# A decoder trunk's FFNs: beginning each down pass with the up pass's last pair, straight from SBUF

## Chip, cores, metric

One core of a Trainium2 chip runs the whole program as one launch. The metric is the device time of that core in microseconds (us), the median of several executions.

## What is computed

One decoder layer for 1024 prompt tokens and 64 sample tokens of width 1024, all in float32: a SwiGLU feed-forward network (FFN) with 2816 hidden columns, a mixer of four gated-MLP groups and four mLSTM heads, and a second FFN, each followed by a layer norm over a scaled residual.

```python
def swiglu(x, wg, wu, wd):
    return (jax.nn.silu(x @ wg) * (x @ wu)) @ wd

def decoder_layer(x, conv_buf, C0, n0, m0, prm):
    x = layer_norm(ALPHA * x + 0.5 * swiglu(x, f1_wg, f1_wu, f1_wd), ln1_g, ln1_b)
    z = x @ w_in + b_in
    u, v, q, k, vm, o, ig, fg = jnp.split(z, SPLIT_POINTS, axis=-1)
    gm, vn = chunk_gmlp(gelu(u), gelu(v), gm_ln_g, gm_ln_b, gm_ws, gm_bs)
    qk = jax.nn.silu(causal_dwconv(concat([conv_buf, q, k]), conv_w, conv_b, T))
    h_ml, C, n, m = mlstm_chunkwise(q, k * ML_HD ** -0.5, vm, ig, log_sigmoid(fg), C0, n0, m0)
    h_ml = jax.nn.sigmoid(o) * h_ml
    mix = concat([head_rms(gm, gm_out_g), head_rms(h_ml, ml_out_g)])
    x = layer_norm(ALPHA * x + mix @ w_out, ln2_g, ln2_b)
    x = layer_norm(ALPHA * x + 0.5 * swiglu(x, f2_wg, f2_wu, f2_wd), ln3_g, ln3_b)
    return x, (vn's last rows, new conv buffer, C, n, m)
```

## The kernel before

**Operands.** A float32 operand is split into two parts, a rounded one (`hi`) and the rest (`lo`); a product takes three matmuls (hi·hi, hi·lo, lo·hi). `split` does this with a cast on ScalarE (ACT, L236) and a subtraction on VectorE (DVE, L237). Both passes of an FFN are multiplied by a Strassen-like scheme of seven block products, called 1 to 7, in the orders `UP_ORDER` and `DOWN_ORDER`, which need sums of blocks beside the blocks themselves.

**Up pass.** The 2816 hidden columns are 11 pairs of 256. For each pair (`Up.step`) the seven products run in order, 24 matmuls of 512 columns each (L379), with four small groups for the sample tokens (L395). The raw up weights come through six slots of the pool `u2` (tag `raw`), three steps ahead; `_prepare` splits them into `uop` (L370, L371). A pair's finished hidden tiles (`c`) are turned by `out` into the seven left operands of the down pass: each is split into a staging tile `hw` (two buffers) and written to DRAM (`hd`, L495, on ACT's queue). `out_sample` does the same for the sample tokens (`hsd`). Both are background generators: `bg.tick()`, called within the matmul loops, advances each of them by one step (to its next `yield`).

**Down pass.** The 11 pairs are taken in four chunks, `CHUNKS` (2, 3, 2 and 4 pairs). In a chunk a round is one product `m` over four row blocks `i` (products 5 and 3, or in the last chunk 7 and 4, share one), each a sum over the chunk's pairs (L703). Left operands `hop` are loaded back from `hd` (`hop_load`, L582) by SyncE (SP), right operands `wop` are made from the down weights `wd` (two pairs in a group of 2 MB) by POOL (block sums), ACT and DVE, a few items ahead (`prepare`, `fetch`). Results are added by DVE to the residual `y` (`add`, L674), which is loaded at the start of the pass (`load_y`, L658). There are four large PSUM buffers (`psum_z`) and four others (`psum_s`).

**The seam.** While the last pair (10) is in the up pass, `early` loads the first weight group and the first seven left operands of pairs 0 and 1 into two tiles (`hop0`, `hop1`) of the pool `xap`, whose slots up operands have left; `prepare(4)` makes four weight operands. After the last step, `up_main` runs the background until pair 10's operands are all written. Then `down` opens the pool `ud` (eight slots `hop`, three `wop`) over the space that was the up pass's. The transposes for the sample's operand of pair 10 wait until `st["down"]` is set, in round 2.

**Order.** The program's order is a priority: a scheduler at compile time fixes the order on each engine by modelled times, and each engine then works its queue strictly in order.

**Mixer.** Background generators again: `gates` (decay and stabiliser of all heads, with the matmul `pdec`, L1096), `mlstm(h)` (starts when `conv` of its head is done; loop over nine row blocks, first matmul L1238; at the end four state products `p3`, L1268, whose operand `vmk` is made by POOL, L1263) and `gmlp`. The filler between their steps are projections (L910, L930), which tick every 6 or 12 matmuls. `Weights` splits the projections' weights on ACT and, for part of them, on POOL (L123).

Of the kernel before, what the change touches and what calls it, by code (L numbers as in the profile page):

```python
# [10 lines left out]
F32 = mybir.dt.float32  # L11
# [5 lines left out]
P = 128  # L17
# [28 lines left out]
NPRE = 2  # L46
CHUNKS = ((0, 1), (2, 3, 4), (5, 6), (7, 8, 9, 10))
PROD = ((0, 0), (0, 1), (1, 0))
# [134 lines left out]
def trunk_kernel(ctx: ExitStack, tc: tile.TileContext, a):  # L183
# [133 lines left out]
    class Up:  # L317


        def __init__(self, ffn, u2, xo, xs):  # L320
            self.ffn, self.u2, self.xo, self.xs = ffn, u2, xo, xs
            self.ct = self.stg = None
            self.steps = [(p, m) for p in range(NPRE) for m in (1, 2)]
            self.steps += [(p, m) for p in range(NPRE) for m in UP_ORDER[2:]]
            self.steps += [(p, m) for p in range(NPRE, NPAIR) for m in UP_ORDER]
            self.prepared = self.loaded = 0
            self.ops, self.raw, self.s1 = {}, {}, {}
            self.x, self.w, self.c, self.smp = {}, {}, {}, {}
# [75 lines left out]
        def step(self, i):  # L404
# [40 lines left out]
            if m == 4:  # L445
                bg.spawn(("hs", self.ffn, p), self.out_sample(p))
                bg.spawn(("h", self.ffn, p), self.out(p))
            bg.tick()

        def out_sample(self, pair):  # L450

            ps = self.smp.pop(pair)
            sm = up_.tile([P, 512], F32, tag="r", name="sm", bufs=4)
            S.copy(sm[:TS], ps[TS:P])
            V.tensor_add(sm[:TS], sm[:TS], ps[:TS])
            yield
# [6 lines left out]
            while pair == NPAIR - 1 and st.get("down") != self.ffn:  # L463
                yield
            pt = psum_s("tp")[:, 0:3 * TS].rearrange("p (f c) -> p f c", f=3)
            for f in range(3):
                TE.transpose(pt[:, f], smv[:, f % 2, f // 2], ident[:TS, :TS])
            hs = sm[:, 0:384].rearrange("p (f s c) -> p f s c", f=3, s=2)
            S.copy(hs[:, :, 0].bitcast(F32R), pt)
            V.tensor_sub(hs[:, :, 1].bitcast(F32R), pt, hs[:, :, 0])  # L470
            yield
            nc.sync.dma_start(hsd[self.ffn][pair], sm[:, 0:384])

        def out(self, pair):

            c = self.c.pop(pair)

            a11, a12, a21, a22 = c["11", 0], c["21", 0], c["12", 0], c["22", 0]
            s1 = None
            for n, m in enumerate(DOWN_ORDER):  # L480
                if m == 6:
                    s1 = self.ctile("s1")
                    V.tensor_add(s1, a21, a22)
                    V.tensor_sub(a21, a21, a11)
                    V.tensor_sub(a11, s1, a11)
                    yield
                if m == 3:
                    V.tensor_sub(a12, a12, a11)
                src = {1: a11, 2: a12, 6: a11, 5: s1, 3: a12, 7: a21, 4: a22}[m]
# [6 lines left out]
                yield  # L496

    def x_operands(xo, rx, rxp):
# [30 lines left out]
    def up_pools(ffn):  # L529

        xsp = tc.alloc_tile_pool(name=f"xs{ffn}", bufs=1, side="right")
        u2 = tc.alloc_tile_pool(name=f"u2{ffn}", bufs=2, side="right")
        rxp = tc.alloc_tile_pool(name=f"rx{ffn}", bufs=1, side="right")
# [5 lines left out]
    def up_main(up, pools, xbp, dn, xops):  # L539
# [7 lines left out]
        stg = tc.alloc_tile_pool(name=f"stg{up.ffn}", bufs=2, side="right", reuse_waits="tile")  # L547
        up.ct, up.stg = ctp, stg
# [7 lines left out]
        for pool in (stg, ctp, u2, xsp, xbp):  # L556
            pool.release()


    class Down:  # L560


        def __init__(self, ffn):
# [3 lines left out]
            self.raws, self.t1s, self.ops, self.hsl, self.hops = {}, {}, {}, {}, {}  # L567
            self.ud = self.hopx = None

# [15 lines left out]
        def early(self):  # L585

            self.load(0)
            h0, h1 = xa_tile(xap, "hop0"), xa_tile(xap, "hop1")
            units = [h0[:, 0], h0[:, 1], h0[:, 2], h1[:, 0], h1[:, 1], h1[:, 2], h1[:, 3]]
            for hop, (_, m, pair) in zip(units[:3], self.items):  # L590
                self.hop_load(hop, pair, m)
            for j, pair in enumerate(CHUNKS[0]):
                hs = h0[:, 3].rearrange("p s c -> p (s c)")[:, j * 384:(j + 1) * 384]
                self.hsl[pair] = hs.rearrange("p (a c) -> p a c", a=3)
                nc.sync.dma_start(hs.bitcast(F32), hsd[self.ffn][pair])
            for hop, (_, m, pair) in zip(units[3:], self.items[3:]):
                self.hop_load(hop, pair, m)
            self.fetched = len(units)

        def fetch(self, upto):  # L600
            while self.fetched < min(upto, len(self.items)):
                ci, m, pair = self.items[self.fetched]
                if ci == len(CHUNKS) - 1 and m == 7:
                    if self.hopx is None:
                        self.hopx = xa_tile(xap, "hopx")
                    hop = self.hopx[:, pair - CHUNKS[-1][0]]
                else:
                    hop = unit(self.ud, "hop", f"hop{pair}_{m}")
                self.hop_load(hop, pair, m)
                self.fetched += 1  # L610

        def prepare(self, upto):
            while self.n < min(upto, len(self.items)):
                i = self.n
                ci, m, pair = self.items[i]
                self.n += 1
                self.load(pair // 2)
                if i >= 8:
                    self.load(pair // 2 + 1)
                b = pair % 2  # L620
                raw = self.raws[pair // 2]
                b11, b12, b21, b22 = raw[:, 2 * b, 0], raw[:, 2 * b, 1], raw[:, 2 * b + 1, 0], raw[:, 2 * b + 1, 1]
                if self.ud is not None:
                    self.fetch(i + 1 + HOP_AHEAD)
                    if m == 1:
                        self.hs_load(pair)
# [33 lines left out]
    def down(dn, residual, on_tile):  # L660
        ffn, ops, hsl, prepare = dn.ffn, dn.ops, dn.hsl, dn.prepare
        y = st["y"]
        ud = tc.alloc_tile_pool(name=f"ud{ffn}", bufs=8, side="right", reuse_waits="tile")
        st["ud"] = dn.ud = ud
        dn.fetch(9)
        load_y(residual, range(4), (0, 1))
# [12 lines left out]
        for ci, pairs in enumerate(CHUNKS):  # L679
# [48 lines left out]
            for r, round_ in enumerate(rounds):  # L728
                ms = sorted({m for m, i in round_}, key=DOWN_ORDER.index)
                done[0] += len(pairs) * len(ms)  # L730
                prepare(done[0] + DOWN_AHEAD)
                if ci == 0 and r == 2:
                    st["down"] = ffn
                if ci == 0 and r == 1:
                    load_y(residual, range(4, 8), (1,))
                    load_y(residual, (8,), (0, 1))
                if ci == 0 and r == 3:
                    load_y(residual, range(4, 8), (0,))
                late = ci == 0 and r < 2

# [52 lines left out]
                for m in ms:  # L793
                    for pair in pairs:
                        dn.hops.pop((pair, m))
        ud.release()

    def fold_tail(sums8):

        y = st["y"]  # L800
        sh = st["ud"].tile([TS, D], F32, tag="hop", name="sh", bufs=8)
        S.copy(sh, y[TS:P, 8, 0:D])
# [190 lines left out]
    def gates():  # L993
# [98 lines left out]
        for h in range(H):  # L1092
            V.tensor_scalar(dd[:, h, :], dmask, dec[:TS, 8, h:h + 1], None, op0=ALU.mult)
        yield
        pd = psum_s("pdec")
        TE.matmul(pd[:, 0:32], lhsT=tri[:TS, P - 1:P].to_broadcast([TS, P]), rhs=dd.rearrange("p h b -> p (h b)"),  # L1096
# [70 lines left out]
    def mlstm(h):  # L1167
        while ("conv", "k", h) not in bg.finished:
            yield
        q, k = conv_out[("q", h)], conv_out[("k", h)]  # L1170
# [90 lines left out]
        for g in range(4):  # L1261
            vmk = m2.tile([TS, 2, P], F32, tag="og", name="vmk")
            G.tensor_tensor(vmk, vx(8)[:, 0:P].unsqueeze(1).to_broadcast([TS, 2, P]),  # L1263
                            bmask[:, 2 * g:2 * g + 2].unsqueeze(2).to_broadcast([TS, 2, P]), op=ALU.mult)
            for _ in range(2):
                yield
# [344 lines left out]
def _layout(v):  # L1611
# [88 lines left out]
```

## Time and profile before

| | |
|---|---|
| median of 3 executions | 1992.83 us (1989.7 to 1997.86) |
| profiled execution | 1990.98 us |
| its span | 1989.2 us |
| TensorE (PE) busy | 1939.1 us, 97% |
| VectorE (DVE) busy | 1318.4 us, 66% |
| ScalarE (ACT), GpSimd (POOL) busy | 764.0 us, 482.9 us |
| seam of the first FFN | around 482 us |
| seam of the second FFN | around 1730 us |
| mixer between them | from about 744 to 1250 us |

How to read the rows. A timeline row gives start, length, engine, line, operation, output and inputs, shapes, count, and in brackets how long the engine had been idle before and what ended that. Rows of waits give engine, tile and line, what was waited for, total us, times, longest. Rows of windows give the stretch, its length, busy time and instructions of PE, PE's weight loads, DVE, ACT, POOL, then the clock that PE was granted (1.00 is full), DMA share and GB/s. Rows of the chain that ended last give start, length and what ran.

### The profile page before, as it was taken

The numbers are of one execution on the slowest core, as the hardware profiler recorded it, in microseconds if no ns is written. First come the engines' busy times: TensorE is split into PE (matmuls) and PEld (weight loads), VectorE is DVE, ScalarE is ACT, GpSimd is POOL, SyncE is SP. The second block draws the span as 40 slices with busy tenths as digits, with TensorE's granted clock in tenths as the row PEclk, the third lists the DMA queues.
The fourth block names the chain that finished last, engine by engine and source line by source line (L and its number), as shares of the span: only waits on it lengthen the run. The fifth ranks groups of instructions, "written<-read, shape, count | busy, mean of one in ns | idle before, by whom it ended". The sixth has DMA issues, their size and how long they took to land.

```text
span 1989.2 us, 27420 instructions
## 1 busy us (share of the span) xinstructions
PE 1939.1 (97%) x10263; PEld 1643.8 (83%) x10263; DVE 1318.4 (66%) x2317; ACT 764.0 (38%) x1499; POOL 482.9 (24%) x404
## 2 busy tenths in 40 slices
PE   8999999999999999999999999999999999989997
PEld 6888888887788889888978999888888888868886
DVE  8865556565756495367775866986565656675757
ACT  6544444443212152154444333544444444321222
POOL 0222222222423031104422400112222222142302
PEclk9999999999999999999999999999999999999999
DMA  5444443338876542111111163244444433897643
GB/s 212 152 160 151 150 142 121 121 128 324 345 264 225 190 141 76 43 35 58 50 36 56 56 219 110 88 152 149 155 149 141 140 120 110 310 350 260 237 150 131
DMA packets 105501, 308.64 MB, mean 155 GB/s; under 512 B 19736, under 2 KB 27416, under 8 KB 102552
## 3 DMA queue, kind: packets, MB, share of 16 engines
q1 hardware_dynamic: 83192, 226.13, 34.3%
q10 hardware_dynamic: 22176, 80.75, 10.1%
q8 instruction: 81, 1.33, 0.3%
q14 instruction: 52, 0.43, 0.1%
HBM read 205.50 MB, written 101.34 MB: 154 GB/s over the span
## 4 chain that ended last, share of the span: by engine, by line
PE 52%; DVE 5%; DMA 2%; POOL 2%; issue 1%; ACT 1%; ACTq 0%; DVEq 0%; POOLq 0%
PE px L379 11%; PE pw L379 6%; PE pd L703 5%; PE pgm L910 4%; PE pq L930 4%; PE pw L703 4%; PE pw L910 4%; PE pz L379 3%; PE pv L910 2%; PE psm L395 2%; PE po L910 2%; DMA hd<-hw 2%; PE psm L712 1%; PE tp L250 1%; DVE yb L305 1%
## 5 line engine op out<-in xcount | busy, mean ns | idle before, releaser
L379 PE MATMUL px<-xo,uop 128*128 128x512 f32 x2112 | 504.1, 394 | 6.0 <-ACT uop L370 5.9
L379 PEld LDWEIGHTS px<-xo,uop 128*128 128x128 f32 x2112 | 392.1, 188 | 91.3 <-ACT uop L370 6.1
L371 DVE TENSOR_TENSOR uop<-ur,uop 128x512 fp32r<-128x512 f32 x264 | 187.5, 731 | 102.9 <-ACT uop L370 102.7
L379 PE MATMUL pw<-xo,uop 128*128 128x512 f32 x1056 | 250.0, 392 | 0.0
L703 PE MATMUL pd<-wop,hop 128*128 128x512 f32 x960 | 233.6, 400 | 8.4 <-ACT wop L236 6.1
L379 PEld LDWEIGHTS pw<-xo,uop 128*128 128x128 f32 x1056 | 198.1, 188 | 44.4
L703 PEld LDWEIGHTS pd<-wop,hop 128*128 128x128 f32 x960 | 182.5, 191 | 53.2 <-ACT wop L236 7.0
L703 PE MATMUL pw<-wop,hop 128*128 128x512 f32 x792 | 190.0, 397 | 7.0 <-DVE yb L674 7.0
L370 ACT CAST uop<-ur 128x512 fp32r<-128x512 f32 x264 | 156.9, 620 | 95.8 <-PE psm L395 65.6
L703 PEld LDWEIGHTS pw<-wop,hop 128*128 128x128 f32 x792 | 148.8, 189 | 43.5 <-DVE yb L674 7.9
L236 ACT CAST wop<-wd 128x512 fp32r<-128x512 f32 x132 | 79.9, 619 | 244.7 <-DVE ya L674 93.8
L360 POOL TENSOR_TENSOR s<-ur,ur 128x1024 f32<-128x1024 f32 x18 | 43.2, 2400 | 511.6 <-DVE uop L371 414.0
L237 DVE TENSOR_TENSOR hw<-c,hw 128x512 fp32r<-128x512 f32 x132 | 107.9, 817 | 81.7 <-ACT hw L236 81.7
L379 PE MATMUL pz<-xo,uop 128*128 128x512 f32 x528 | 128.1, 398 | 0.0
L237 DVE TENSOR_TENSOR wop<-wd,wop 128x512 fp32r<-128x512 f32 x132 | 110.8, 852 | 24.5 <-ACT wop L236 23.8
L236 ACT CAST hw<-c 128x512 fp32r<-128x512 f32 x132 | 82.0, 621 | 112.4 <-DMA hd<-hw 50.6
L379 PEld LDWEIGHTS pz<-xo,uop 128*128 128x128 f32 x528 | 97.4, 188 | 22.8 <-DVE uop L371 0.4
L395 PEld LDWEIGHTS psm<-uop,xs 128*128 128x128 f32 x704 | 95.3, 189 | 7.8 <-ACT uop L370 0.3
L910 PE MATMUL pgm<-w,xt 128*128 128x256 f32 x768 | 99.1, 286 | 0.0
L910 PE MATMUL pw<-w,xt 128*128 128x256 f32 x768 | 97.3, 284 | 1.0 <-ACT xt L236 1.0
L395 PE MATMUL psm<-uop,xs 128*128 128x256 f32 x704 | 97.9, 281 | 0.0
L930 PE MATMUL pq<-xt,w 128*128 128x512 f32 x384 | 96.7, 403 | 0.0
(328 smaller groups left out, 2867.2 us busy)
## 6 DMA issues: line engine op xcount, KB each, us to landing
hd<-hw ACTq DMA_DIRECT2D x154, 512.0 KB, 3.4
hop<-hd SPq DMA_DIRECT2D x146, 512.0 KB, 5.0
ur<-in_wu SPq DMA_DIRECT2D x94, 512.0 KB, 3.9
wd<-in_wd SPq DMA_DIRECT2D x22, 1024.0 KB, 8.0
wr<-in_ws SPq DMA_DIRECT2D x76, 256.0 KB, 2.8
hsd<-sm SPq DMA_DIRECT2D x22, 192.0 KB, 4.1
hopx<-hd SPq DMA_DIRECT2D x8, 512.0 KB, 5.5
hs<-hsd SPq DMA_DIRECT2D x18, 192.0 KB, 7.4
```

Of the source, the lines that this page charges most:

```text
L236: S.copy(hi, src)
L237: V.tensor_sub(dst[ix + (1,)], src, hi.bitcast(F32))
L250: TE.transpose(pv[:, j, :rows], y[:rows, t, c0:c0 + P], ident[:rows, :rows])
L305: V.scalar_tensor_tensor(yt, yt, mv[:rows, 2:3], b_t[:rows], op0=ALU.mult, op1=ALU.add)
L360: eng.tensor_tensor(s1, a21, a22, op=ALU.add)
L370: S.copy(op[:, 0], sj)
L371: V.tensor_sub(op[:, 1], sj, op[:, 0].bitcast(F32))
L379: TE.matmul(ps, lhsT=units[k // 2][:, wi, c0:c0 + P], rhs=self.xo[m][:, k, xi, :], start=start and k == 0 and j == 0, stop=k == 3 and j == ...
L395: TE.matmul(ps, lhsT=self.xs[:, which, k, :], rhs=units[k // 2][:, wi, (k % 2) * 256:(k % 2 + 1) * 256], start=first and k == 0 and wi == ...
L703: TE.matmul(p, lhsT=hop[:, hi, i * P:(i + 1) * P], rhs=wop[:, wi, :], start=start and pi == 0 and j == 0, stop=pi == len(pairs) - 1 and j ...
L910: TE.matmul(p[:, :n], lhsT=xl(t, k, xi), rhs=wk[:, wi, kk * n:(kk + 1) * n], start=(i == 0), stop=(i == last - 1))
L930: TE.matmul(p[:, :n], lhsT=wk[:, wi, kk * P:(kk + 1) * P], rhs=rhs, start=(i == 0), stop=(i == (23 if c < 2 else 15)), skip_group_check=c ...
```

## The change

The chunks are regrouped so that the first holds pairs 0 and 10. Pair 10's seven left operands are not written to DRAM: `out_last` splits them straight into the tiles `hop0` and `hop1`, the first while the up pass still runs, the others after its last step. Its sample operand is split into the end of `hop1`. The up weights' six `raw` slots stay allocated through the down pass and are, with three slots of `ud`, the ring for loaded left operands (before: eight slots of `ud`); pair 0's operands come through them (`early_hops`). The down weights are ordered on the host by the new sequence of pairs. In the first chunk the sample products 1 and 2 move from round 1 to round 2, and `st["down"]` is set in round 1. Three matmuls of the mixer are issued some background steps later: `pdec` four steps, a head's first matmul three, each of its four `p3` two.

```diff
-CHUNKS = ((0, 1), (2, 3, 4), (5, 6), (7, 8, 9, 10))
+CHUNKS = ((0, 10), (1, 2, 3), (4, 5), (6, 7, 8, 9))
+DORD = tuple(p for pairs in CHUNKS for p in pairs)
+LAST = NPAIR - 1
...
# Up.step, after the last product of a pair
-                bg.spawn(("h", self.ffn, p), self.out(p))
+                if p < LAST:
+                    bg.spawn(("h", self.ffn, p), self.out(p))
+                else:
+                    self.complete = True
...
# Up.out_sample
+            if pair == LAST:
+                split(self.dn.hsl[LAST].rearrange("p f (s c) -> p f s c", s=2), 2, pt)
+                return
...
# Up.out now loops over hidden_operands(c), which holds the sums it made itself
+        def out_last(self):
+            for m, src in self.hidden_operands(self.c[LAST]):
+                split(self.dn.hops[(LAST, m)], 1, src)
+                yield
+                while not self.complete:
+                    yield
...
# up_pools: u2 is now allocated ahead of xsp; up_main no longer releases it
             up.step(i)
-            if up.steps[i] == (NPAIR - 1, 6):
+            if up.steps[i] == (LAST, 6):
                 dn.early()
-            elif up.steps[i] == (NPAIR - 1, 3):
+                bg.spawn(("h", up.ffn, LAST), up.out_last())
+            elif up.steps[i] == (LAST, 7):
+                dn.early_hops()
+            elif up.steps[i] == (LAST, 3):
                 dn.prepare(4)
...
# Down.early: seven units of hop0 and hop1 become hops[(LAST, m)]; the last unit holds the samples' operands
+        def early_hops(self):
+            self.fetch(4)
+            nc.sync.dma_start(self.hsl[0].bitcast(F32).rearrange("p a c -> p (a c)"), hsd[self.ffn][0])
+            self.fetch(12)
...
# Down.fetch
                 ci, m, pair = self.items[self.fetched]
+                self.fetched += 1
+                if pair == LAST:
+                    continue
...
-                    hop = unit(self.ud, "hop", f"hop{pair}_{m}")
+                    self.ring += 1
+                    if self.ud is not None and self.ring % 3 == 0:
+                        hop = unit(self.ud, "hop", f"hop{pair}_{m}")
+                    else:
+                        hop = unit(self.u2, "raw", f"hop{pair}_{m}", 6)
...
# Down.prepare: weight groups by DORD
-                self.load(pair // 2)
+                group, b = divmod(DORD.index(pair), 2)
+                self.load(group)
...
# down
-        ud = tc.alloc_tile_pool(name=f"ud{ffn}", bufs=8, side="right", reuse_waits="tile")
+        ud = tc.alloc_tile_pool(name=f"ud{ffn}", bufs=3, side="right", reuse_waits="tile")
-        dn.fetch(9)
+        dn.fetch(14)
...
-                if ci == 0 and r == 2:
+                if ci == 0 and r == 1:
                     st["down"] = ffn
-                if ci == 0 and r == 1:
                     load_y(residual, range(4, 8), (1,))
                     load_y(residual, (8,), (0, 1))
...
-                late = ci == 0 and r < 2
+                late = ci == 0 and r < 3
...
-                    samples(() if late and r == 0 else (1, 2) if late else ms)
+                    samples(() if late and r < 2 else (1, 2) if late else ms)
...
         ud.release()
+        dn.u2.release()
...
# gates, ahead of pdec
+        for _ in range(4):
+            yield
...
# mlstm, at its start; and ahead of each p3
+        for _ in range(3):
+            yield
...
-            for _ in range(2):
+            for _ in range(4):
                 yield
...
# host
-        wd[f].reshape(24, P, D)[:NF] = w[f"ffn{f + 1}_wd"].reshape(NF, P, D)
+        wd[f].reshape(24, P, D)[:NF] = w[f"ffn{f + 1}_wd"].reshape(NPAIR, 2, P, D)[list(DORD)].reshape(NF, P, D)
```

More of the change, by code (lines that the diff above doesn't have):

```diff
@@ L462, in out_sample @@
                 yield
-            while pair == NPAIR - 1 and st.get("down") != self.ffn:
+            while pair == LAST and st.get("down") != self.ffn:
                 yield
@@ L476, in out @@
             c = self.c.pop(pair)
[L478 to L489, printed above, removed]
+            for n, (m, src) in enumerate(self.hidden_operands(c)):
                 hop = unit(self.stg, "stg", f"hw{pair}_{m}", 2)
@@ L496, in out, with hidden_operands @@
                 yield
+        def hidden_operands(self, c):
+            a11 = c["11", 0]
+            yield 1, a11
+            a12, a21, a22 = c["21", 0], c["12", 0], c["22", 0]
+            yield 2, a12
+            s1 = self.ctile("s1")
+            V.tensor_add(s1, a21, a22)
+            V.tensor_sub(a21, a21, a11)
+            V.tensor_sub(a11, s1, a11)
+            yield 6, a11
+            yield 5, s1
+            V.tensor_sub(a12, a12, a11)
+            yield 3, a12
+            yield 7, a21
+            yield 4, a22
+        def out_last(self):
[4 more added lines that the diff above has]
+                    yield
     def x_operands(xo, rx, rxp):
@@ L547, in up_main @@
         stg = tc.alloc_tile_pool(name=f"stg{up.ffn}", bufs=2, side="right", reuse_waits="tile")
-        up.ct, up.stg = ctp, stg
+        up.ct, up.stg, up.dn, dn.u2 = ctp, stg, dn, u2
         for i in range(i + 1, len(up.steps)):
             up.step(i)
-            if up.steps[i] == (NPAIR - 1, 6):
+            if up.steps[i] == (LAST, 6):
                 dn.early()
-            elif up.steps[i] == (NPAIR - 1, 3):
+                bg.spawn(("h", up.ffn, LAST), up.out_last())
+            elif up.steps[i] == (LAST, 7):
+                dn.early_hops()
+            elif up.steps[i] == (LAST, 3):
                 dn.prepare(4)
         bg.until(("h", up.ffn, NPAIR - 1))
-        for pool in (stg, ctp, u2, xsp, xbp):
+        for pool in (stg, ctp, xsp, xbp):
             pool.release()
@@ L567, in __init__ @@
             self.raws, self.t1s, self.ops, self.hsl, self.hops = {}, {}, {}, {}, {}
-            self.ud = self.hopx = None
+            self.ud = self.hopx = self.u2 = None
+            self.fetched = self.ring = 0
         def load(self, group):
@@ L588, in early @@
             h0, h1 = xa_tile(xap, "hop0"), xa_tile(xap, "hop1")
-            units = [h0[:, 0], h0[:, 1], h0[:, 2], h1[:, 0], h1[:, 1], h1[:, 2], h1[:, 3]]
-            for hop, (_, m, pair) in zip(units[:3], self.items):
-                self.hop_load(hop, pair, m)
+            units = [h0[:, j] for j in range(4)] + [h1[:, j] for j in range(3)]
+            for hop, m in zip(units, DOWN_ORDER):
+                self.hops[(LAST, m)] = hop
+            hs = h1[:, 3].rearrange("p s c -> p (s c)")
             for j, pair in enumerate(CHUNKS[0]):
[L593 to L598, printed above, removed]
+                self.hsl[pair] = hs[:, j * 384:(j + 1) * 384].rearrange("p (a c) -> p a c", a=3)
+        def early_hops(self):
+            self.fetch(4)
+            nc.sync.dma_start(self.hsl[0].bitcast(F32).rearrange("p a c -> p (a c)"), hsd[self.ffn][0])
+            self.fetch(12)
         def fetch(self, upto):
@@ L616, in prepare @@
                 self.n += 1
-                self.load(pair // 2)
+                group, b = divmod(DORD.index(pair), 2)
+                self.load(group)
                 if i >= 8:
-                    self.load(pair // 2 + 1)
-                b = pair % 2
-                raw = self.raws[pair // 2]
+                    self.load(group + 1)
+                raw = self.raws[group]
                 b11, b12, b21, b22 = raw[:, 2 * b, 0], raw[:, 2 * b, 1], raw[:, 2 * b + 1, 0], raw[:, 2 * b + 1, 1]
@@ L624, in prepare @@
                     self.fetch(i + 1 + HOP_AHEAD)
-                    if m == 1:
+                    if m == 1 and pair not in self.hsl:
                         self.hs_load(pair)
@@ L796, in down @@
         ud.release()
+        dn.u2.release()
     def fold_tail(sums8):
         y = st["y"]
-        sh = st["ud"].tile([TS, D], F32, tag="hop", name="sh", bufs=8)
+        sh = st["ud"].tile([TS, D], F32, tag="hop", name="sh", bufs=3)
         S.copy(sh, y[TS:P, 8, 0:D])
```

4 lines of the change are left out of this document (2 added, 2 removed).

## The prediction

> **What bounds the kernel now.** I read the page's busy shares first, then what TensorE waited for, then its timeline where the waits sit, then what the engines it waited for were doing.
>
> ```profile
> span 1989.2 us, 27420 instructions
> PE 1939.1 (97%) x10263; PEld 1643.8 (83%) x10263; DVE 1318.4 (66%) x2317; ACT 764.0 (38%) x1499; POOL 482.9 (24%) x404
> ...
> PE pw L703 <- DVE yb L674: 7.0, 2, 4.5
> PE pd L703 <- ACT wop L236: 6.1, 2, 3.3
> ...
> PE pd L703 <- DVE wop L237: 2.0, 2, 1.0
> ```
>
> TensorE (PE) is the bound: 97% busy, some 50 us idle. The change leaves the count of matmuls as it is, so all it can win is idle time and the slow matmuls behind idle time. The three L703 rows, 15.1 us, come twice each: once in each seam, where a down pass follows an up pass. This is PE's timeline at the second seam, with the first and last row of the same stretch at the first:
>
> ```profile
> 1737.10 4.33 PE L703 MATMUL pw<-wop,hop 128*128 128x512 f32 x18
> 1745.97 2.47 PE L703 MATMUL pw<-wop,hop 128*128 128x512 f32 x6 [4.54 <-DVE yb L674]
> 1748.24 1.48 PE L703 MATMUL pd<-wop,hop 128*128 128x512 f32 x3
> 1749.65 0.50 PE L467 MATMUL tp<-cc,sm 64*128 64x64 f32 x3
> 1750.09 2.35 PE L703 MATMUL pd<-wop,hop 128*128 128x512 f32 x9
> 1752.28 2.95 PE L703 MATMUL pw<-wop,hop 128*128 128x512 f32 x12
> 1758.06 0.50 PE L703 MATMUL pd<-wop,hop 128*128 128x512 f32 x1 [2.83 <-ACT wop L236]
> 1759.55 4.37 PE L703 MATMUL pd<-wop,hop 128*128 128x512 f32 x11 [0.99 <-DVE wop L237]
> 1763.79 6.52 PE L703 MATMUL pw<-wop,hop 128*128 128x512 f32 x27
> ...
> 489.80 4.34 PE L703 MATMUL pw<-wop,hop 128*128 128x512 f32 x18
> ...
> 514.87 8.49 PE L703 MATMUL pw<-wop,hop 128*128 128x512 f32 x36
> ...
> 1832.52 16.65 PE pd L703 x72
> ```
>
> From 1737.10 to 1763.79 run 60 full matmuls and 3 transposes in 26.7 us. At the pace of the last row, an undisturbed stretch on the chain that ended last (16.65 / 72 = 0.231 us), they need 13.9 + 0.4 us. So the second seam loses 12.4 us: 8.4 of waiting and 4.0 of slow matmuls (11 in 4.37 us are 0.40 each). The first has the same 60 matmuls between 489.80 and 514.87: 25.1 − 14.3 = 10.8 us lost. Together **23.2 us**.
>
> Why the waits? The operands of the up pass's last pair, pair 10, are split into `hw` (2 buffers) and written to DRAM. The view of tile hw over 1729 to 1764 lists who sat idle before it, then come single rows of ACT's and DVE's timelines:
>
> ```profile
>   DMA hd<-hw: 12.4, 4
>   ACT hw L236: 5.5, 2
> ...
> 1743.38 0.62 ACT L236 CAST hw<-cs 128x512 fp32r<-128x512 f32 x1 [6.82 <-DMA hd<-hw]
> 1757.39 1.66 ACT L236 CAST wop<-wd 128x512 fp32r<-128x512 f32 x3 [0.61 <-DVE hw L237]
> ...
> 1745.24 0.68 DVE L674 SCALAR_TENSOR_TENSOR yb<-yb,psm 128x512 f32<-128x512 f32 x1
> ```
>
> ACT stands 6.82 us behind a write that has to leave a staging buffer; DVE stands behind ACT, 5.5 us in two waits; the eviction at 1745.24 that PE needs (4.54 us) stands behind DVE. The second wait has the same root: the casts of three weight operands at 1757.39 start when the last `hw` split has ended, because their slots lie where the last hidden tiles were.
>
> **The change, part by part.** *Last pair from SBUF.* Per pass it removes 7 writes of `hd`, 7 loads of `hop`, one write and one load of the sample's operand, and the wait for the two staging buffers. The 7 splits stay on ACT and DVE, unstaged; the one for product 1 moves ahead into the up pass. With the staging gone, the 12.4 us that ACT stood behind writes go, and with them both causes above. The upper bound is all 23.2 us.
>
> *What is late next: DVE.*
>
> ```profile
> 1729.68:1763.79 34.11, 25.74 (x97) 19.14 (x95) 26.36 (x39) 11.05 (x20) 13.63 (x10) 0.90 0.86 304
> ```
>
> The columns are length, PE, PEld, DVE, ACT, POOL, clock, DMA share, GB/s. DVE works 26.36 us in 34.11. Without PE's loss the same matmuls take 21.7 us. The split of product 1 (0.69) leaves the stretch, and of the weight splits those of products 7 and 4 (four of 0.69) can be done later, for they are two rounds away: 22.9 us are left for 21.7. Evictions may trail by the eight PSUM buffers, which speaks for no stall; the order of DVE's queue, written by the compiler, for some. So the residue lies between 0 and the whole present loss. I take 3 us in each seam, near the 1.2 us of excess and half of it slow clock, and keep 0 and 9 for the range. Seams: 23.2 − 6 = **17.2 us**.
>
> *Products 1 and 2 of the samples one round later, their transposes one round earlier.* The same matmuls; one of the four small PSUM buffers is free in round 1, which was the one PE waited for at 1745.97. The transposes take one back. Counted in the residue.
>
> *Ring of nine slots (six of the up weights, three new) for eight.* Early loads for pair 0 wait for the up weights' last casts. Covers:
>
> ```profile
> 1718.62 1.29 DVE L371 TENSOR_TENSOR uop<-ur,uop 128x512 fp32r<-128x512 f32 x2 [1.54 <-ACT uop L370]
> ...
> hop<-hd SPq DMA_DIRECT2D x146, 512.0 KB, 5.0
> ...
> 1723.43 3.64 SPq L658 DMA_DIRECT2D ya<-x2d x8
> ```
>
> The last up cast ends at 1719.9, a hop lands 5.0 us later at 1724.9, and the down pass begins at 1729.68: 4.8 us of cover for even the last of them, and that one is wanted only two rounds on. They are out of SP's queue before the loads of y at 1723.43, which wait for an operand of the up pass anyway. The operand of pair 0's product 4 reuses the first slot and waits for round 0; it is wanted in the last round of the chunk. Zero, with that cover. The 14 fewer writes and 14 fewer loads lie beside PE's work: zero. The reordered down weights and `fold_tail`'s slot cost nothing: same sizes, same rounds.
>
> *Mixer.* Three matmuls come some background steps later.
>
> ```profile
> 763.07 11.37 PE pv L910 x96
> ...
> 797.39 0.38 PE L1096 MATMUL pdec<-gtmp,cc 64*128 64x32 f32 x2 [3.21 <-DVE gtmp L1093]
> 797.70 14.55 PE L910 MATMUL pv<-w,xt 128*128 128x256 f32 x108
> ...
> 1038.87 0.46 PE L1238 MATMUL p<-cq,ck 128*128 128x128 f32 x2 [2.00 <-DVE ck L1163]
> 1079.99 0.70 PE L1268 MATMUL p<-vmk,kw 64*128 64x256 f32 x2 [2.79 <-POOL vmk L1263]
> 1080.61 3.55 PE L910 MATMUL pgm<-w,xt 128*128 128x256 f32 x16
> 1087.14 0.70 PE L1268 MATMUL p<-vmk,kw 64*128 64x256 f32 x2
> ...
> 1137.67 1.47 PE L910 MATMUL pw<-w,xt 128*128 128x256 f32 x6 [1.00 <-ACT xt L236]
> ...
> 1041.00:1047.00 6.00, 6.00 (x27) 5.61 (x26) 1.17 (x4) 0.58 (x2) 0.00 (x0) 0.52 0.00 0
> ```
>
> `pdec`: 3.21 of waiting, then 108 matmuls in 14.55 where 0.118 each (11.37 / 96) gives 12.8: 5.0 us. Its 4 steps are 12 matmuls each, 5.7 us, more than the wait; all goes, and the next user of its result is a whole head away. First matmul of the head's loop (L1238): 2.00, and the last row, of the stretch behind it, has six microseconds at a granted clock of 0.52, half lost: 2.9 more, 4.9. Its 3 steps of 6 matmuls are 2.1 us, barely the wait: 3.5. `vmk` (L1268): 2.79, then 16 matmuls in 3.55 for 1.9: 4.4 us. Two steps are 1.4 us, and its engine was behind other work:
>
> ```profile
> 1076.28 3.08 POOL L123 TENSOR_TENSOR w<-wr,w 128x512 fp32r<-128x512 f32 x2 [3.15 <-ACT w L121]
> ...
> 930.71 0.79 PE L1238 MATMUL p<-cq,ck 128*128 128x128 f32 x2 [1.40 <-DVE wt L1216]
> ```
>
> So 2.5. Delaying four heads moves every chain against PE's filler; one new wait like the last row, 1.4 us with as much slow clock behind it, with even odds or better: −2. A head gets 3 + 8 steps longer, under 10 us; head 3's last `vmk` matmul was at 1087, the output projection starts at 1137.67: covered. Mixer: 5.0 + 3.5 + 2.5 − 2 = **9 us**, bounds −3 (five such new waits) and 14.3. With a head move its state's load and its stores on SP (no one waits for the stores, and the load is asked for eight steps before its last row block) and its POOL operands against the weight splits of L123; that is the 1.9 us held back for `vmk`.
>
> *Slow clock.* That half clock came behind a wait of only 2.00 us. So I price a short residual wait at twice its length. The Trainium skill, TensorE: Matmul & The Clock Gate, "Why this matters for your kernels", asks only that idle gaps stay under some 3 us. By that rule the residues (1.5 us of idle in each seam) would carry no clock loss, the sum would be 3 us more, and the time 1964; the 0.52 behind 2.00 us differs from it, and I go by the row.
>
> **Sum.** 17.2 + 9 = 26.2 us. The profiled execution took 1990.98 us (span 1989.2 and 1.8 around it): 1964.8. The median of the runs shown, 1992.83, lies 1.85 above it: 1966.6, rounded to **1967**.
>
> **Rivals.** (a) *DVE takes the place of the staging.* For it: 22.9 us of work for 21.7 on one in-order queue, with weight splits ahead of evictions. Against it: DVE still idled 5.5 us for ACT there. With a residue of 8 in each seam, 23.2 − 16 + 9 = 16: 1977. (b) *Everything goes.* 23.2 + 14.3 = 37.5: 1955. For it: one cause under both waits. Against: DVE's balance. (c) *It doesn't do what it says:* the weight slots still wait for pair 10's hidden tiles, or the loads of pair 0 come late, and only the mixer gains: 9 less, down to nothing: 1984 to 1993. For it: the new pool lies over the same tiles as the row at 1757.39; against: the splits no longer wait for writes.
> (d) *Slower: the load of the next weights stands behind operand loads in SP's one queue.*
>
> ```profile
> 1785.21 0.62 PE L712 MATMUL psm<-wop,hs 128*128 128x512 f32 x2
> ...
> 1777.70 1.14 ACT L236 CAST wop<-wd 128x512 fp32r<-128x512 f32 x2 [4.18 <-DMA wd<-in_wd]
> ...
> wd<-in_wd SPq DMA_DIRECT2D x22, 1024.0 KB, 8.0
> ```
>
> A ring load now waits for PE to free an old slot, and weights queue behind it. They arrived at 1777.7 for a chunk whose first matmuls run at 1785.2, 7.5 us ahead; it decides when they come more than 7.5 us later against PE. If each of six chunk changes then cost a landing of 8.0 us, +48 − 26 = +22: 2015. Against it: nine slots where there were eight, and the same order of rounds.
>
> **How the numbers follow.** The forecast holds 0.58 (1958 to 1976 by its residues of 0 to 6 and mixer of 5 to 12), (b) 0.10, (a) 0.18, (c) 0.09, (d) 0.05. The range, 1953 to 1985, takes in (b), (a) and the edge of (c). About 0.5%, 10 us, is what a measurement tells from no change: below 1983 lie the forecast, (b) and nearly all of (a), 0.84; (c) and the rest of (a), 0.11; (d), 0.05.
>
> **What would show it.** Right: no idle row before L703 above 1.5 us in either seam, no casts waiting for `hd` writes from the last step of the up pass on, 60 matmuls at that place in 14 to 18 us, no `pdec` wait. Wrong: a wait of 3 us or more for `wop`, `y` or `hop` in rounds 1 to 3, new waits at a chunk's start (d), or new waits of several us on mixer tiles.

## The result, and the profile after

The changed kernel took 1966.58 us (median of five executions, 1964.74 to 1967.1), the kernel before 1991.28 on the same chip (five, 1989.54 to 1997.86). The ratio is 0.987, with a 95% interval of 0.9851 to 0.9888. The profiled execution took 1967.1 us. From here on, "after" is the changed kernel. The first two parts of its page:

```profile
span 1965.3 us, 27416 instructions
PE 1929.7 (98%) x10263; PEld 1637.7 (83%) x10263; DVE 1322.3 (67%) x2317; ACT 767.7 (39%) x1501; POOL 480.8 (24%) x404
```

The count of matmuls is the same. To see where 23.9 us of span went, cut both timelines of TensorE at the same instructions: the first matmul of each down pass, the first sample matmul of its second chunk (a "seam" lies between these two), the first matmul of the gates and the last of `pmix` (the mixer lies between these two).

| us | up pass 1 | seam 1 | to the gates | mixer | to down pass 2 | seam 2 | rest |
|---|---|---|---|---|---|---|---|
| before | 482.40 | 53.80 | 238.08 | 373.56 | 581.84 | 55.53 | 203.99 |
| after | 483.30 | 46.77 | 238.06 | 364.61 | 581.81 | 46.75 | 204.00 |

The seams gave 15.8 us and the mixer 9.0; the first up pass took 0.9 back (the same stretch varies from 482.1 to 484.1 over all kernels run here). The three other stretches agree within 0.03 us: no chunk change and no later round pays for the new ring.

After, the waits of TensorE that answer to the three L703 rows of before, and those of the mixer:

```profile
PE pd L737 <- ACT wop L238: 2.6, 2, 1.3
PE p L1285 <- DVE wt L1254: 2.4, 1, 2.4
PE pmix L1396 <- POOL ge L1387: 1.8, 1, 1.8
PE p L1276 <- DVE ck L1199: 1.6, 1, 1.6
...
PE pw L737 <- DVE hop L239: 1.5, 2, 0.8
PE pd L737 <- DVE wop L239: 1.5, 2, 0.7
```

At the seams 15.1 us of waiting became 5.6. In the mixer the waits for `pdec`'s input and for `vmk` (3.2 and 3.6 before) are gone; the one for `wt`, now at L1285, has grown from 1.8 (1.4 and 0.4 in two places before) to 2.4, and `ge` at L1396 is new. After, TensorE's timeline at the second seam:

```profile
1720.13 0.86 PE L737 MATMUL pw<-wop,hop 128*128 128x512 f32 x3
1720.93 0.40 PE L473 MATMUL tp<-cc,sm 64*128 64x64 f32 x3
1721.25 3.75 PE L737 MATMUL pw<-wop,hop 128*128 128x512 f32 x15
1726.30 1.61 PE L737 MATMUL pd<-wop,hop 128*128 128x512 f32 x6 [1.30 <-ACT wop L238]
1728.65 1.21 PE L737 MATMUL pd<-wop,hop 128*128 128x512 f32 x4 [0.74 <-DVE wop L239]
1730.61 1.65 PE L737 MATMUL pw<-wop,hop 128*128 128x512 f32 x6 [0.75 <-DVE hop L239]
1732.11 2.02 PE L746 MATMUL psm<-wop,hop 128*128 128x512 f32 x8
1733.96 3.43 PE L737 MATMUL pd<-wop,hop 128*128 128x512 f32 x14
1737.23 2.95 PE L737 MATMUL pw<-wop,hop 128*128 128x512 f32 x12
```

Up to 1737.23 run 56 full matmuls and the three transposes in 17.1 us. At the prediction's pace (0.231 us each, 0.4 for the transposes) they need 13.3, so 3.8 us are still lost here, where 12.4 were lost before; 2.79 of it is the three idle times. The same stretches by windows (both seams' front is alike; here the first seam whole, its front, then the mixer):

```profile
483.30:530.07 46.77, 43.94 (x190) 34.44 (x188) 43.50 (x60) 14.41 (x26) 28.75 (x19) 1.00 0.86 316
483.30:505.92 22.62, 19.79 (x85) 14.98 (x84) 22.62 (x32) 9.50 (x18) 13.92 (x9) 1.00 0.79 271
768.13:1132.74 364.61, 354.70 (x2478) 322.27 (x2476) 244.41 (x620) 146.43 (x409) 108.64 (x155) 0.98 0.17 48
```

In the seam's front DVE is busy 22.62 of 22.62 us: two of TensorE's three waits there are for an engine that never stops. The first and longest is for ACT.

### The profile page after: what moved, and what is told of

Same layout as the page of the kernel before. It is cut to its first block, busy times and chain, and to the rows that moved or that the text cites. A ratio compares the mean times of both kernels' runs of the same rounds, so it can differ in the third digit from the quotient of the medians.

```text
span 1965.3 us, 27416 instructions
## 1 busy us (share of the span) xinstructions
PE 1929.7 (98%) x10263; PEld 1637.7 (83%) x10263; DVE 1322.3 (67%) x2317; ACT 767.7 (39%) x1501; POOL 480.8 (24%) x404
## 3 DMA queue, kind: packets, MB, share of 16 engines
q8 instruction: 81, 1.33, 0.3%
## 4 chain that ended last, share of the span: by engine, by line
PE 51%; DVE 6%; POOL 2%; ACT 1%; issue 1%; DMA 1%; SPq 0%; DVEq 0%; ACTq 0%; POOLq 0%
PE px L382 12%; PE pw L382 6%; PE pd L737 5%; PE pw L737 4%; PE pw L944 4%; PE pq L964 4%; PE pz L382 3%; PE pv L944 3%; PE psm L398 2%; PE po L944 2%; PE pgm L944 1%; PE psm L746 1%; PE tp L252 1%; POOL grs L244 1%; DVE yb L307 1%
## 5 line engine op out<-in xcount | busy, mean ns | idle before, releaser
L737 PE MATMUL pd<-wop,hop 128*128 128x512 f32 x960 | 228.3, 394 | 4.4 <-ACT wop L238 2.6
L239 DVE TENSOR_TENSOR hw<-c,hw 128x512 fp32r<-128x512 f32 x120 | 96.5, 804 | 69.8 <-ACT hw L238 68.9
L238 ACT CAST hw<-c 128x512 fp32r<-128x512 f32 x120 | 74.4, 620 | 73.5 <-DVE c L504 45.4
L944 PEld LDWEIGHTS pgm<-w,xt 128*128 128x128 f32 x768 | 95.4, 193 | 5.4 <-issue 3.5
```

The costliest lines, as they stand in the source:

```text
L238: S.copy(hi, src)
L239: V.tensor_sub(dst[ix + (1,)], src, hi.bitcast(F32))
L737: TE.matmul(p, lhsT=hop[:, hi, i * P:(i + 1) * P], rhs=wop[:, wi, :], start=start and pi == 0 and j == 0, stop=pi == len(pairs) - 1 and j ...
L944: TE.matmul(p[:, :n], lhsT=xl(t, k, xi), rhs=wk[:, wi, kk * n:(kk + 1) * n], start=(i == 0), stop=(i == last - 1))
```

## Experiments: the two halves

**seam_only** is after without the three mixer delays.

```diff
# gates, mlstm start, ahead of each p3
-        for _ in range(4): yield
-        for _ in range(3): yield
-            for _ in range(4): yield
+            for _ in range(2): yield
```

> The changed kernel without the three later mixer matmuls. If the two parts add up, only the seams are gained: the stretch from the end of the first FFN to the output projection takes its old time (9 us more than in the changed kernel), each seam loses about 3.7 us instead of 10.8 and 12.4, and the time is 1975 to 1976. If instead the mixer's waits went because the seam shifted the mixer's transfers, the time stays near 1967.

**mixer_only** is before with those delays alone (the same lines the other way round).

> The kernel before with the three later mixer matmuls alone. If the parts add up: the seams keep their 23 us, the mixer gains 9 us, 1982. If the mixer's gain needs the other half of the change: 1988 to 1992.

Measured on one chip, before at 1993.14 us: seam_only 1979.31, ratio 0.9927 (0.9912 to 0.9942); mixer_only 1981.42, ratio 0.9938 (0.9923 to 0.9953). That is 14.5 and 12.4 us, together 26.9, where the whole change gave 1.3% or 25.9: the halves add up. In the profiles seam_only's seams are 46.74 and 46.76 us and mixer_only's mixer is 364.20, each as in after. The other half has the code of before, but not quite its times: mixer_only's seams are 56.27 and 54.21. The split by times, 14.5 to 12.4, is nearer to even than the 15.8 to 9.0 of the two profiles; part of the reason stands in one window row, the mixer of seam_only, which is the code of before:

```profile
767.21:1144.64 377.43, 361.78 (x2477) 328.46 (x2475) 245.38 (x620) 144.95 (x407) 113.26 (x155) 0.96 0.16 47
```

and the mixer of before:

```profile
774.28:1147.84 373.56, 358.40 (x2477) 325.19 (x2476) 244.98 (x620) 144.76 (x407) 112.36 (x155) 0.97 0.17 47
```

TensorE is idle nearly as long in both (length less PE's busy time: 15.65 and 15.16). The same matmuls were 3.4 us slower in one execution than in the other, so a single pair of profiles is a poor measure. All the profiles of this case say more. The three with the old mixer (these two and stg3) have it at 373.56 to 377.43 us, with TensorE busy for 358.40 to 361.78; the eight with the three delays have it at 363.03 to 364.61, busy for 352.40 to 354.70. The means are 11.7 us apart, close to the 12.4 by times: 4.9 of it is idle time and 6.8 is faster matmuls. Before's mixer is the shortest of its three and after's the longest of its eight, so 9.0 is the low end.

## Experiments: why the seam's waits go

**stg3** gives before a third staging buffer and nothing else.

```diff
-                hop = unit(self.stg, "stg", f"hw{pair}_{m}", 2)
+                hop = unit(self.stg, "stg", f"hw{pair}_{m}", 3)
-        stg = tc.alloc_tile_pool(name=f"stg{up.ffn}", bufs=2, side="right", reuse_waits="tile")
+        stg = tc.alloc_tile_pool(name=f"stg{up.ffn}", bufs=3, side="right", reuse_waits="tile")
```

> The kernel before, with three staging buffers for the written operands instead of two (all that the memory holds). If the seam's loss comes from ACT standing behind writes that have to leave a buffer, one more buffer lets one operand more through ahead of each wait: ACT's waits for hd writes between the pass's start and 34 us after it fall from 12.4 us to 5 to 9, and each seam (53.8 and 55.5 us from the down pass's first matmul to chunk 1) gets 3 to 7 us shorter. If DVE's work or the loads hold the seam, it stays within 1 us.

Measured in one execution: 1990.55 us against 1993.71, seams 53.76 and 54.15 us. The 3 to 7 us did not come: over before, mixer_only and the three kernels with one delay, the old seam varies from 52.92 to 56.39, so these two show no gain. The view of tile `hw` at the second seam says that ACT's idle time behind writes fell by a third, from 12.4 us:

```profile
  DMA hd<-hw: 8.3, 2
```

TensorE's waits over the first seam of stg3:

```profile
PE tp L467 <- DVE ya L674: 2.7, 1, 2.7
PE pw L703 <- DMA hop<-hd: 2.5, 1, 2.5
PE pd L703 <- ACT wop L236: 1.2, 1, 1.2
```

The wait for `wop` fell from 3.3 us to 1.2, as the theory of a staging cause has it. The wait of 2.5 in round 1 is gone with the sample products still in that round, but one of 2.7 for an eviction stands soon after it, at the transposes. And behind them stands a wait that before does not show: 2.5 us for the load of `hop` from DRAM (3.2 at the second seam). In this kernel pair 10 belongs to the last chunk, so this load is of pairs 0 and 1. It came late because SP stood behind a staged write of pair 10. These are SP's wait (from the view of the first seam), ACT's issue of the last such write, and the loads, the first of `hop` since 465:

```profile
SPq L582 <- DMA hd<-hw: 5.4, 1, 5.4
503.80 0.33 ACTq L495 DMA_DIRECT2D hd<-hw  x1
509.73 11.43 SPq L582 DMA_DIRECT2D hop<-hd  x9
```

So the staged writes held up SP's queue beside ACT's and DVE's, and a third buffer leaves that in place. In after neither ACT nor SP waits for a write of `hd` in either seam. With two thirds of the staging wait left, stg3 is no clean measure of the staging, and no run takes the staged writes away while the sample products stay in round 1, or the other way round. That the seam half's gain comes from the staged writes is shown by who waits for whom before and after, not by a run that changes nothing else.

**writes_back** leaves that order alone and only puts 14 writes back: after, plus a write of pair 10's operands to DRAM that nobody reads.

```diff
-                split(self.dn.hops[(LAST, m)], 1, src)
+                hop = self.dn.hops[(LAST, m)]
+                split(hop, 1, src)
+                c0 = DOWN_ORDER.index(m) * 1024
+                nc.scalar.dma_start(hd[self.ffn][LAST][:, c0:c0 + 1024], hop.bitcast(F32).rearrange("p s c -> p (s c)"))
```

> The changed kernel, and pair 10's seven operands are also written to DRAM again, from the tiles in SBUF that nobody has to reuse at once (nobody reads the copies). If what cost the time was the wait for a staging buffer, 14 more writes change nothing: 1967, within 1 us in each seam. If it was the traffic itself (the transfers' share of the 16 engines, late loads of y or weights), most of the 15.8 us of the two seams come back: 1978 to 1983.

Measured: 1964.30 us, ratio 0.9859 (0.9839 to 0.9879), not slower than after. Its first seam by windows:

```profile
482.70:528.02 45.32, 43.68 (x190) 34.42 (x188) 42.29 (x59) 14.52 (x26) 27.80 (x19) 1.00 0.97 383
```

The DMA engines are fuller than in after (0.97 against 0.86, 383 GB/s against 316), and the seam is 1.4 us shorter. So the traffic of the writes is worth nothing here; that of the loads, which this run leaves out, was not put back. What counted was that engines waited for the writes. Why the seam is shorter, where within 1 us was expected, is not settled; with the extra writes the compiler ordered ACT's and DVE's queues differently.

## Experiments: what is left of the seam

The first of after's waits is for ACT's cast of a weight operand. These are rows of after's timelines of POOL, ACT and DVE at the first seam:

```profile
487.60 2.75 POOL L665 TENSOR_TENSOR t<-wd 128x512 f32<-128x512 f32 x1 [3.68 <-ACT hop L238]
490.43 1.62 POOL L666 TENSOR_TENSOR wd<-wd,t 128x512 f32<-128x512 f32 x1
...
492.08 1.14 ACT L238 CAST wop<-wd 128x512 fp32r<-128x512 f32 x2 [1.71 <-POOL wd L666]
...
489.14 3.46 DVE L239 TENSOR_TENSOR hop<-c,hop 128x512 fp32r<-128x512 f32 x2
```

POOL's block sum waits 3.68 us for a slot in which ACT still reads a hidden tile, then runs beside DVE's subtractions and both are slow: two in 3.46 us.

**t1_own** gives that sum a tile of its own.

```diff
-                    t1 = up_.tile([P, 512], F32, tag="r", name="t1", bufs=4)
+                    t1 = spare if pair == LAST else up_.tile([P, 512], F32, tag="r", name="t1", bufs=4)
```

> The changed kernel; the block sum t1 of pair 10's weights (product 6) goes to a tile of its own instead of a slot of the ring r, for which POOL stands idle 3.7 us at the seam until pair 10's last use of another slot. If the remaining 3.7 us of each seam hang on this chain (slot, two block sums on POOL, cast, subtraction), POOL starts it 3 us earlier, the two waits for wop (2.0 us in each seam, and slow matmuls behind) go, and the time is 1961 to 1963. If DVE's load is what holds the seam, as the prediction has it, nothing moves: 1966 to 1967.

Measured: 1962.86 us, ratio 0.9845 (0.9829 to 0.9862), seams 45.37 and 45.22: 1.4 and 1.5 us less than after. Its rows at the first seam (POOL, DVE, then TensorE):

```profile
484.47 1.75 POOL L670 TENSOR_TENSOR wd<-wd 128x512 f32<-128x512 f32 x1
494.07 1.30 POOL L665 TENSOR_TENSOR t<-wd 128x512 f32<-128x512 f32 x1 [7.85 <-DVE ya L708]
...
490.83 1.27 DVE L239 TENSOR_TENSOR hop<-c,hop 128x512 fp32r<-128x512 f32 x2
...
490.96 0.28 PE L473 MATMUL tp<-cc,sm 64*128 64x64 f32 x1 [0.99 <-DVE sm L466]
497.94 1.66 PE L737 MATMUL pw<-wop,hop 128*128 128x512 f32 x6 [0.75 <-DVE hop L239]
```

POOL's sums are done by 486.2, DVE's two subtractions fall from 3.46 to 1.27 us, and in the first seam both waits for `wop` are gone, for a new one of 0.99 at the transposes. Of the 3.8 us lost in after's first seam, 1.4 went with this slot; on top of the next edit (both against tp_late, below) the same change is worth 1.8 and 2.1. But the slot is not the only way to these 1.4: writes_back's seams are as short, 45.32 and 45.38, with no wait for `wop`, and there POOL still stands idle 3.68 us ahead of the same sum. Another order of ACT's and DVE's queues went with as much.

**tp_late** moves the sample transposes and the sample products one round later again, and **both** is t1_own with that edit. The theory was that the transposes hold one of the small PSUM buffers too early.

```diff
-                if ci == 0 and r == 1:
+                if ci == 0 and r == 2:
                     st["down"] = ffn
...
-                    samples(() if late and r < 2 else (1, 2) if late else ms)
+                    samples(() if late else ms)
+                elif ci == 0:
+                    samples((1, 2))
```

> The changed kernel; the transposes of pair 10's sample operand and the sample products 1 and 2 come one more round later, so that in round 1 all four small PSUM buffers belong to product 2. If the wait of 0.8 us at the end of round 1 is for the buffer that the transposes hold (their copy stands 6 us deep in DVE's queue), it goes, and with it some slow clock: each seam 0.8 to 1.5 us shorter than 46.8. If DVE's queue as such is late, the wait only changes its name: 46 to 47.

> The changed kernel with both: block sum t1 of pair 10 in a tile of its own, and transposes and sample products 1 and 2 one more round later. The pace of 0.231 us gives the seam stretch 43.0 us without any loss. If slot, POOL chain and transposes were the whole residue, the seams come down to 43 to 44 and the time to 1959 to 1961. If DVE's 22.9 us of work for 21.7 us of matmuls holds the rest, evictions (y) or splits (wop) become what PE waits for and the seams stay at 44.5 to 45.4: 1961 to 1963.

Measured: tp_late 1972.63 us, ratio 0.9892 (0.9877 to 0.9907); both 1968.72, ratio 0.9868 (0.9851 to 0.9884). The theory falls: the seams get longer, 49.20 and 49.60 in tp_late, 47.39 and 47.52 in both, some 2 to 3 us each more than without the move. TensorE's waits over tp_late's first seam:

```profile
PE tp L473 <- DVE ya L708: 1.5, 1, 1.5
PE pd L737 <- DVE wop L239: 1.2, 1, 1.2
```

and that seam by windows:

```profile
484.14:533.34 49.20, 45.99 (x189) 36.23 (x188) 44.27 (x59) 14.34 (x26) 28.70 (x19) 0.93 0.83 300
```

A round later the transposes stand behind an eviction (`ya`), where after has no wait. Against after's first seam only 0.4 of the 2.4 us is idle time (3.21 against 2.83); 2.05 is slower matmuls, at a clock of 0.93 where after had 1.00. Here the price of the longer waits is nearly all slow clock. Both kernels also lose 1.8 us between the mixer and the second down pass, at no wait that the profile shows; that stays open.

**pool_hops** is t1_own with three of DVE's seven subtractions for pair 10 given to POOL, which idles.

```diff
+                if m in (3, 7, 4):
+                    S.copy(hop[:, 0], src)
+                    G.tensor_sub(hop[:, 1], src, hop[:, 0].bitcast(F32))
+                else:
+                    split(hop, 1, src)
```

> The version with pair 10's block sum t1 in its own tile (seams 45.3 us, DVE busy without a gap from the down pass's first matmul on), and the three subtractions of pair 10's operands for products 3, 7 and 4 on POOL, which stands idle for 7.9 us there. If DVE's full queue is what the rest of the residue hangs on, 1.9 us of its work less make each seam 1 to 2 us shorter, 43.5 to 44.3, and the time 1959 to 1961. If not (POOL beside DVE slows both, or the transposes' buffer is what counts), the seams stay at 45 to 46.

Measured: 1965.15 us, ratio 0.9855 (0.9838 to 0.9871), seams 46.05 and 47.00: no better than t1_own. The second seam's waits:

```profile
PE pw L742 <- DVE yb L713: 1.5, 2, 0.8
PE tp L473 <- DVE sm L466: 1.0, 1, 1.0
PE tp L473 <- DVE sm L465: 0.6, 1, 0.6
```

TensorE waits for three other results of DVE, but DVE was not relieved: it is busy 42.20 and 43.57 us of the two seams, where t1_own has 42.40 in each. Only two of the three subtractions had stood in the seam, and others took longer beside POOL's (the one for `sm` at L465 took 1.50 us for 0.41). So this run does not test a lighter DVE, and whether DVE's load or its order sets the last 2.1 to 2.4 us of a seam stays open. Each try renamed the tile that is late in DVE's queue; what order would clear it was not found.

**after_again** is the changed kernel, unchanged, in one more execution.

> The changed kernel once more, for its mixer stretch (364.6 us, 9.9 of it PE idle). The idle part should repeat within 0.5 us. If what else differs between kernels in the mixer is where the clock happens to be throttled after a wait, PE's busy time there (354.7 us) moves by 1 to 5 us with nothing changed; if it is the program, it repeats too.

1966.95 us, seams 48.29 and 46.74. The first seam has after's waits to 0.03 us, and is 1.5 us longer. Its last wait and what follows, on TensorE's timeline, and a window of about the same length as the one of after's front:

```profile
499.20 2.48 PE L737 MATMUL pw<-wop,hop 128*128 128x512 f32 x6 [0.76 <-DVE hop L239]
501.48 2.80 PE L746 MATMUL psm<-wop,hop 128*128 128x512 f32 x8
```

```profile
483.19:505.92 22.73, 19.91 (x79) 14.98 (x78) 21.33 (x30) 9.23 (x17) 13.88 (x9) 0.92 0.79 268
```

The same 14 matmuls took 1.66 + 2.02 us in after's first seam and take 2.48 + 2.80 here, at a mean clock of 0.92 instead of 1.00. Those 1.6 us ride on whether the clock falls behind an equal wait. The mixer, for which the run was made, took 363.09 us for 364.61: TensorE was busy 2.3 us less there (352.40) and idle 0.8 more (10.69), so the idle time did not quite repeat within the 0.5 that was expected.

## Experiments: the three delays in the mixer, one at a time

Each is before with one delay: **m_pdec** (four steps ahead of `pdec`), **m_start** (three at a head's start), **m_vmk** (two more ahead of each `p3`). One execution each, before at 1993.71 us.

> The kernel before, with pdec alone four steps later. The prediction priced it at 5.0 us (3.2 of waiting, 1.8 of slow matmuls behind): the wait for gtmp goes, no other mixer wait changes, the mixer's stretch falls from 373.6 to 368 to 370 us. If delays only shift waits, another wait of 2 to 3 us appears and the stretch stays at 371 to 374.

> The kernel before, with each head's first matmul alone three steps later. Prediction: 3.5 us from the wait for ck, stretch 370. In the changed kernel that wait still stands with 1.6 of its 2.0 us: if the steps alone leave it so, the gain is 0.4 us of idle time and whatever the clock does behind it: 371 to 374, and new waits of the heads' chains (wt, pmix) show whether these three steps bring them.

> The kernel before, with each of the four state products alone two steps later. Prediction: 2.5 us, as part of a 2.8 us wait behind POOL's weight splits remains; stretch 371. In the changed kernel no wait for vmk is left, so by that 3.6 us of idle time and some slow clock go: 368 to 370.

Measured: 1984.38, 1984.86 and 1992.47 us. Their mixers by windows, in that order, one fence for each kernel:

```profile
775.81:1143.87 368.06, 357.50 (x2477) 323.87 (x2475) 245.01 (x620) 144.77 (x407) 112.31 (x155) 0.97 0.16 47
```

```profile
777.92:1144.43 366.51, 352.21 (x2478) 320.64 (x2476) 243.74 (x620) 147.16 (x409) 110.38 (x155) 0.99 0.17 48
```

```profile
776.54:1151.98 375.44, 360.74 (x2477) 326.77 (x2475) 246.37 (x620) 143.89 (x407) 111.80 (x155) 0.97 0.16 46
```

The stretches are 5.5 and 7.1 us shorter and 1.9 longer than before's 373.56. But TensorE's idle time in them (length less busy) is 10.6, 14.3 and 14.7 against 15.2: only `pdec` takes much of it, 4.6. The rest is PE's busy time. In m_vmk it lies among those of the three old mixers (358.40 to 361.78), so nothing can be read from it; in m_start it is 6.2 us below the lowest of them, more than they differ among themselves, and the stretch is shorter than the 370 to 374 that were expected. The waits say where. m_start:

```profile
PE p L1249 <- DVE wt L1218: 2.7, 2, 1.6
...
PE p L1240 <- DVE ck L1163: 0.6, 1, 0.6
```

m_vmk:

```profile
PE pmix L1358 <- POOL ge L1349: 1.8, 1, 1.8
...
PE p L1268 <- POOL vmk L1263: 0.9, 1, 0.9
```

m_start takes 1.4 of the 2.0 us at the head's first matmul; before waited 1.8 for `wt` (1.4 at L1238 and 0.4 at L1247), m_start 2.7. m_vmk takes 2.7 of 3.6 and pays 1.8 at `pmix`, where nothing was. Both trade a wait for one further on. What m_start gains beyond waits is clock. Behind the wait for `ck`, 2.0 to 2.2 us long, the next eight microseconds had a granted clock of 0.57 in before, 0.79 in seam_only, 1.00 in stg3, 0.79 in m_pdec and 0.57 in m_vmk. In m_start (0.6 us left) and in all eight profiles with the three delays (1.6 left) it is 1.00. The rows of before and of after:

```profile
1038.87:1046.87 8.00, 8.00 (x34) 6.87 (x35) 2.50 (x9) 2.11 (x7) 0.60 (x1) 0.57 0.00 0
1024.37:1032.37 8.00, 8.00 (x62) 7.39 (x63) 5.38 (x17) 3.06 (x11) 1.42 (x3) 1.00 0.00 0
```

m_pdec trades nothing: its wait of 3.2 is gone, the list is else that of before to 0.3 us, save that `tp` behind `ya` waited 0.5 instead of 1.5, in this one execution.

## Why the prediction was right, step by step

**The seam.** Predicted 17.2 us with a residue of 3 in each seam; measured 15.8 with 3.8 and 3.6 (46.77 and 46.75 less the 43.0 and 43.1 that before's seams leave without their loss). The step "what is late next: DVE" holds in kind: DVE works without a gap, and two of the three waits left are for it. That 22.9 us of work were foreseen and 22.62 found is partly luck: 22.62 is the whole window, and in it stand subtractions that POOL slowed (two of 1.73 us where 0.63 would do). Of the signs named, no wait is above 1.33 us and no cast waits for a write of `hd`; 60 matmuls at that place would take some 18.0 us (17.1 for the 56), the upper edge of 14 to 18. Three things in the step were off.
- Its make-up: "half of it slow clock". In the profile of after 2.8 of each residue is idle time, at a clock of 1.00 in both seams.
- "One cause under both waits": the views bear it out, and stg3's late load stood behind a staged write as well. But no run measures the staging alone, and the one that came near, stg3, did not shorten the seams.
- It held that only DVE would be late. A third or more of the residue went with the slot for POOL's sum (t1_own), or with another order of the queues (writes_back). Neither was in the sum.

**The clock.** The prediction priced a short wait by a row of before, in which six microseconds behind a wait of 2.00 us had a clock of 0.52. In after's seams waits of 1.3, 0.7 and 0.8 us left the clock at 1.00; in after_again the same waits went with 0.92 in the first seam, and in tp_late waits of 1.5, 1.2 and 0.5 with 0.93. The Trainium skill, TensorE: Matmul & The Clock Gate, "Why this matters for your kernels", asks only that idle gaps stay under some 3 us. After's seams agree with that; before's row and the first seams of after_again and tp_late, where the clock fell behind shorter gaps, do not. The price by the skill, 1964, missed the median by 2.6 and the row's 1967 by 0.4, but the seams do not decide for the row: their idle time was 2.8 each where both sums took 1.5.

**The ring and the loads at zero.** Held: no wait for a DMA stands in TensorE's list after, and the stretches behind the seams kept their length to 0.03 us. With that rival (d) is out.

**The mixer.** 9 us predicted; 9.0 between the two profiles, 12.4 (9.4 to 15.3) by the times of mixer_only, 11.7 between the means of all profiles. So by all profiles the sum was some 2.7 too small, and more than half of the gain, 6.8 of the 11.7, is faster matmuls. `pdec` at 5.0 is borne out: 4.6 of idle time in m_pdec, 5.5 of length. The head's start at 3.5 took only 0.9 of idle time alone, but the slow clock behind its wait, at which the prediction looked, is gone in all nine profiles with the three steps; m_start, in one execution, is 7.1 us shorter. `vmk` at 2.5 is not borne out: alone it took 0.5 of idle time, and no length. Of the new wait priced at 2, `ge` came with 1.8, and `wt` grew by 0.6.

**Luck in the number.** The forecast took 26.2 us off 1992.83. The result has before at 1991.28 and the gain at 24.7 (25.9 by the ratio), so that 1967 met 1966.58 so closely is partly the base. And the terms missed in opposite directions: the seams gave 1.4 less than the sum, the mixer by all profiles 2.7 more.

**The rivals.** (a) named what most of TensorE's remaining waits at the seam are for, DVE, with 8 where 3.7 came. (b) failed: 3.8 and 3.6 are still lost in the seams. (c) is refuted by seam_only.

## What to carry to other kernels

Where one pass feeds the next through DRAM, begin the next with the piece that is still in SBUF: the gain was not the writes' traffic (writes_back pays for the writes and loses nothing) but queues that no longer stand behind a staged write. After such a change look for the next resource in the same place; here a scratch slot, found by asking what released POOL, gave another 2.9 us over two seams, and t1_own (0.9845) has the lowest median of all, though its interval overlaps with after's. When a matmul is delayed to cover its wait, look for the same wait further along the chain. Read idle time and busy time apart, and over several executions: here a pair of profiles was off by 3 us, where eight against three were clear.

## What the runs showed of the hardware

- One code with nearly equal waits is not one time. Before's mixer and seam_only's differ by 3.4 us of PE's busy time; after's and after_again's first seam by 1.5.
- A wait of 2 us can cost clock, and need not: behind the same wait for `ck`, 2.0 to 2.2 us long, eight microseconds had a granted clock of 0.57, 0.57, 0.79, 0.79 and 1.00 in five kernels. Behind 0.6 to 1.6 us it was 1.00 in nine profiles.
- DVE and POOL slow each other. A DVE subtraction of two SBUF tiles took 0.63 us with POOL idle and 1.73 beside POOL's sums in after. Of those sums the first took 2.75 and the second 1.62, where 1.30 is what one took beside DVE's additions from PSUM (t1_own, 494.07). The Trainium skill, SBUF — State Buffer, "Who interferes with whom", has a DVE instruction with two SBUF inputs contend with a POOL instruction that reads SBUF. The rows agree.
